# Two wider pads that move every tile of one side of the on-chip memory to a multiple of 256 bytes

## The chip, the cores and the metric

The kernel runs on one core of one Trainium2 chip. The metric is the device time of one execution in microseconds (us), as the median of several runs. Beside the runs there is one profiled execution with its trace; its span runs from the first instruction to the last.

## What is computed

One encoder block over 256 tokens of 2048 channels, in float32. Cut to its shape:

```
h = rmsnorm(x);  proj = h @ w_in                       # 2048 -> 9216
p_hy, p_sgu, g_hy, g_sgu = split(proj)
y_hy  = two long convolutions with implicit filters(p_hy)    # 1024 channels
y_sgu = gelu(u) * (w_s applied along chunks of layernorm(gelu(v)))   # 1024 channels
merged = sigmoid(g_hy) * (y_hy @ w_branch_hyena) + sigmoid(g_sgu) * (y_sgu @ w_branch_sgu)
x = x + merged @ w_out                                 # 2048 -> 2048
gate, up = split(rmsnorm(x) @ w_ffn_in)                # 2048 -> 2 x 5632
x = x + (silu(gate) * up) @ w_ffn_out                  # 5632 -> 2048
out = rmsnorm(x)
```

## The kernel before

**Products in parts.** Every weight is read once from HBM, 512 KB at a time, into a tile `raw` of 128 x 1024 float32. `split_to` makes a rounded part `whi` on ScalarE (line 67) and the rest `wlo` on VectorE (line 68). The activations are held split in the same way: `X`, `M`, `X2`, `H`, `ysgu` and `yhy` hold, for each block k of 128 channels, 256 columns of the rounded part and then 256 of the rest. A product is then three matmuls (lines 132 to 134, in `tokens`): 128 columns of an activation tile are the stationary operand, 512 columns of `whi` or `wlo` are streamed past them. One weight tile gives 12 such matmuls. In the projections u, v, x1 and x2 (`tile16`, lines 98 and 100) it is the other way round: `whi` and `wlo` are stationary, and 512 or 256 columns of `X` are streamed.

**Order of the work.** First the half of the spatial gating that is normalized (lines 700 to 702, 192 matmuls), then the gates (`gate_part`, tiles `mg`, in blocks of 24 matmuls) mixed with `tile16`, the filters and the convolutions (lines 512, 561, 596, 617). After that the two branches (`ysgu`, `yhy`), the output projection (`M`), the first feed-forward product (`X2`, which the profile also calls X) and the second (`H`). `feed` loads and splits the weight tiles ahead of their use, all through SyncE's queue.

**Where tiles lie.** Each of the 128 partitions has one row of addresses. A pool is placed from the left end or, with side="right", from the right end, one behind the other, and every tile is rounded up to 32 bytes. The first tile, `par`, begins at byte 16,512. With the sizes in the code this gives, before the change:

| tiles | side | first byte | past a multiple of 256 |
|---|---|---|---|
| `ones`, `ident` | left | 17,152 | 0 |
| `raw`, `whi`, `wlo` in the pool ws | left | 20,352 | 128 |
| `ysgu` and `X2` (the same place) | left | 80,000 | 128 |
| `yhy` | left | 96,384 | 128 |
| `zh`, `zl` (tokens of the convolution) | left | 120,000 | 192 |
| `w4h`, `w4l`, `fh`, `fl` (filters) | right | 157,504 on | 64 |
| `H` | right | 114,624 | 192 |
| `M` | right | 135,104 | 192 |
| `h3s` | right | 195,520 | 192 |
| `X` | right | 196,544 | 192 |
| `raw`, `whi`, `wlo` in the pool ws2 | right | 204,736 | 192 |

Every operand of a matmul begins a multiple of 512 bytes into its tile, so it lies as far past a multiple of 256 as the tile does. The pool ws2 exists only from the branches on; there every third weight tile of the list goes to it:

```python
            pool, n = (self.ws, RAW_BUFS) if self.ws2 is None or i % 3 else (self.ws2, 2)
```

Of the kernel before, what the change touches and what calls it, by code (L numbers as in the profile page):

```python
# [9 lines left out]
F32 = mybir.dt.float32  # L10
# [6 lines left out]
P = 128  # L17
# [199 lines left out]
def build(nc, tc, a):  # L217
# [29 lines left out]
    with ExitStack() as top:  # L247
        const = top.enter_context(tc.tile_pool(name="const", bufs=1))
# [5 lines left out]

        par = const.tile([P, PC_N], F32, name="par")
        nc.scalar.dma_start(out=par, in_=a["par"])
        const.tile([P, 8], F32, name="const_pad")
        ones = net.ones = const.tile([P, P], F32, name="ones")
        nc.vector.memset(ones, 1.0)
        ident = net.ident = const.tile([P, P], F32, name="ident")  # L260
# [2 lines left out]


        edge = top.enter_context(tc.tile_pool(name="edge", bufs=1, side="right"))
        edge.tile([P, 8], F32, name="edge_pad")
        left = ExitStack()
        ys_pool = left.enter_context(tc.tile_pool(name="ys_pool", bufs=1))
        ysgu = ys_pool.tile([P, 8, 512], F32R, name="ysgu")
# [699 lines left out]
```

## Time and profile before

| what | value |
|---|---|
| time, median of 3 runs | 1407.9 us (1407.68 to 1407.92) |
| time of the profiled execution | 1408.45 us |
| its span | 1406.7 us |
| TensorE busy | 1390.8 us, 99% |
| VectorE, ScalarE busy | 870.1 us, 657.3 us |
| granted TensorE clock, mean | 0.998 |

The trace lists every matmul with its start and a modelled end. Since matmuls are pipelined, the shown duration of one overlaps the next one's; what a matmul costs is the distance from its start to the start of the next.

### The profile page before, as it was taken

Reading aid. Unit: us, or ns where it says so; the run is one execution under the profiler, and the core shown is the slowest. Engines: PE = TensorE matmul, PEld = TensorE weight load, DVE = VectorE, ACT = ScalarE, POOL = GpSimd, SP = SyncE. Lnnn points to the kernel's source line nnn. Section 1 sums busy time; section 2 is a strip of 40 time slices with the busy share of each in tenths; the row PEclk is TensorE's granted clock in tenths of the full one; section 3 lists DMA queues with packets and bytes.
Section 4 is the critical chain, followed back from the end, with each engine's and each line's share of the span. In section 5 each row is a group of like instructions: output and inputs, shape, how many; then the busy total and the mean of one; then the engine's idle time right before and its main releaser. Section 6 shows DMA issues by size and latency. Waiting matters only on the chain.

```text
span 1406.7 us, 17274 instructions
## 1 busy us (share of the span) xinstructions
PE 1390.8 (99%) x6554; PEld 1149.7 (82%) x6554; DVE 870.1 (62%) x1206; ACT 657.3 (47%) x820; POOL 0.7 (0%) x6
## 2 busy tenths in 40 slices
PE   9999999999999999999999999999999999999996
PEld 7888888888888788888888888888888888888885
DVE  7787798797888666556555454545454554545443
ACT  7665555555554444445444444444444443434432
POOL 0000000000000000000000000000000000000000
PEclk9999999999999999999999999999999999999999
DMA  8775656556555786677666566666665667666651
GB/s 285 261 223 180 188 166 199 174 170 205 178 171 165 259 312 183 203 223 209 186 188 186 188 192 184 193 181 190 183 193 184 192 230 234 188 187 193 186 173 60
DMA packets 81170, 276.00 MB, mean 196 GB/s; under 512 B 9016, under 2 KB 9664, under 8 KB 80704
## 3 DMA queue, kind: packets, MB, share of 16 engines
q1 hardware_dynamic: 78064, 269.59, 61.8%
q10 hardware_dynamic: 3024, 5.32, 1.0%
q8 instruction: 51, 0.84, 0.2%
q14 instruction: 31, 0.25, 0.1%
HBM read 266.49 MB, written 8.39 MB: 195 GB/s over the span
## 4 chain that ended last, share of the span: by engine, by line
PE 96%; DMA 1%; DVE 1%; ACT 1%; issue 0%; SPq 0%; ACTq 0%; DVEq 0%
PE mm L132 21%; PE mm L134 21%; PE mm L133 21%; PE mm L98 8%; PE mg L132 4%; PE mg L133 4%; PE mg L134 4%; PE mm L100 4%; PE aux L561 2%; PE aux L160 1%; PE aux L617 1%; PE mm L700 1%; PE mm L701 1%; PE mm L702 1%; PE aux L512 1%; DMA raw<-in_wbr 1%
## 5 line engine op out<-in xcount | busy, mean ns | idle before, releaser
L68 DVE TENSOR_TENSOR wlo<-raw,whi 128x1024 fp32r<-128x1024 f32 (+1 forms) x474 | 577.3, 1219 | 478.1 <-ACT whi L67 474.2
L67 ACT CAST whi<-raw 128x1024 fp32r<-128x1024 f32 (+1 forms) x474 | 495.3, 1046 | 627.1 <-PE mm L134 466.8
L132 PE MATMUL mm<-whi,X 128*128 128x512 f32 x704 | 278.8, 396 | 0.0
L134 PE MATMUL mm<-whi,X 128*128 128x512 f32 x704 | 275.8, 392 | 0.0
L133 PE MATMUL mm<-wlo,X 128*128 128x512 f32 x704 | 274.4, 390 | 0.0
L98 PE MATMUL mm<-X,whi 128*128 128x512 f32 x512 | 160.0, 394 | 0.0
L134 PEld LDWEIGHTS mm<-whi,X 128*128 128x128 f32 x704 | 132.1, 188 | 30.4
L133 PEld LDWEIGHTS mm<-wlo,X 128*128 128x128 f32 x704 | 132.3, 188 | 28.4
L132 PEld LDWEIGHTS mm<-whi,X 128*128 128x128 f32 x704 | 132.2, 188 | 27.2
L133 PE MATMUL mm<-wlo,H 128*128 128x512 f32 x352 | 138.5, 393 | 0.0
L132 PE MATMUL mm<-whi,H 128*128 128x512 f32 x352 | 138.4, 393 | 0.0
L134 PE MATMUL mm<-whi,H 128*128 128x512 f32 x352 | 138.1, 392 | 0.0
L100 PEld LDWEIGHTS mm<-X,wlo 128*128 128x128 f32 x512 | 96.1, 188 | 21.5
L132 PE MATMUL mg<-whi,X 128*128 128x512 f32 x256 | 102.1, 399 | 0.0
L100 PE MATMUL mm<-X,wlo 128*128 128x256 f32 x512 | 101.4, 279 | 0.0
L133 PE MATMUL mg<-wlo,X 128*128 128x512 f32 x256 | 101.1, 395 | 0.0
L134 PE MATMUL mg<-whi,X 128*128 128x512 f32 x256 | 100.9, 395 | 0.0
L98 PEld LDWEIGHTS mm<-X,whi 128*128 128x128 f32 x512 | 78.7, 188 | 1.2
L132 PEld LDWEIGHTS mm<-whi,H 128*128 128x128 f32 x352 | 65.9, 187 | 15.7
L133 PEld LDWEIGHTS mm<-wlo,H 128*128 128x128 f32 x352 | 65.9, 187 | 15.6
L134 PEld LDWEIGHTS mm<-whi,H 128*128 128x128 f32 x352 | 65.9, 187 | 15.5
L134 PEld LDWEIGHTS mg<-whi,X 128*128 128x128 f32 x256 | 48.0, 188 | 11.4
(214 smaller groups left out, 1427.6 us busy)
## 6 DMA issues: line engine op xcount, KB each, us to landing
raw<-in_wfi SPq DMA_DIRECT2D x176, 512.0 KB, 3.5
raw<-in_wfo SPq DMA_DIRECT2D x88, 512.0 KB, 3.5
raw<-in_wg SPq DMA_DIRECT2D x64, 512.0 KB, 3.7
raw<-in_win SPq DMA_DIRECT2D x64, 512.0 KB, 3.9
raw<-in_wbr SPq DMA_DIRECT2D x32, 512.0 KB, 5.7
raw<-in_wout SPq DMA_DIRECT2D x32, 512.0 KB, 4.0
raw<-in_wsv SPq DMA_DIRECT2D x14, 512.0 KB, 5.7
gate_d<-sq ACTq DMA_DIRECT2D x16, 256.0 KB, 5.2
```

What stands on the lines that cost most here:

```text
L67: self.nc.scalar.copy(out=hi, in_=src)
L68: self.nc.vector.tensor_tensor(out=lo, in0=src, in1=hi.bitcast(F32), op=ALU.subtract)
L98: nc.tensor.matmul(ps[:, 0:512], lhsT=hi[:, col:col + P], rhs=mov, start=start, stop=False)
L100: nc.tensor.matmul(ps[:, 0:256], lhsT=lo[:, col:col + P], rhs=mov[:, 0:256], start=False, stop=stop)
L132: self.nc.tensor.matmul(ps[tt], lhsT=xh, rhs=wh, start=start, stop=False)
L133: self.nc.tensor.matmul(ps[tt], lhsT=xh, rhs=wl, start=False, stop=False)
L134: self.nc.tensor.matmul(ps[tt], lhsT=xl, rhs=wh, start=False, stop=stop)
L160: self.nc.tensor.transpose(out=pt[:, b, tt * P:(tt + 1) * P], in_=src[tt][:, cols + b * P:cols + (b + 1) * P], identity=self.ident)
L512: nc.tensor.matmul(ps.rearrange("p d c -> p (d c)"), lhsT=h3s[:, par_ * P:(par_ + 1) * P], rhs=w, start=(part == 0), stop=(part == 1))
L561: nc.tensor.matmul(ps[:, ri, :], lhsT=fw[:, m + ri, :], rhs=z, start=(n == 0), stop=(n == 2))
L617: nc.tensor.matmul(ps[:, ri].rearrange("p h t -> p (h t)"), lhsT=p[:, ri, t * P:(t + 1) * P], rhs=GG[:, 2 * gr + ri, :], start=(n == 0), s ...
L700: nc.tensor.matmul(ps[tt], lhsT=xh, rhs=wh, start=(k == 0), stop=False)
```

## The change

The unused tile behind `par` grows from 32 to 160 bytes, and the unused tile at the right end from 32 to 224 bytes. Everything behind the first moves 128 bytes to the right, everything on the right side 192 bytes to the left. No instruction, tile size, pool or order changes.

```diff
-        const.tile([P, 8], F32, name="const_pad")
+        const.tile([P, 40], F32, name="const_pad")
         ones = net.ones = const.tile([P, P], F32, name="ones")
...
-        edge.tile([P, 8], F32, name="edge_pad")
+        edge.tile([P, 56], F32, name="edge_pad")
```

After it ws, `ysgu`, `X2`, `yhy`, ws2, `H`, `M`, `h3s` and `X` begin at multiples of 256 bytes. `ones` and `ident` then lie 128 past one, the filters' tiles 128, and `zh` and `zl` 64.

## Rows read from the trace of the kernel before

**Rows 1.** The page: TensorE's busy time, and shares of the chain that ended last.

```profile
PE 1390.8 (99%) x6554; PEld 1149.7 (82%) x6554; DVE 870.1 (62%) x1206; ACT 657.3 (47%) x820; POOL 0.7 (0%) x6
...
PE 96%; DMA 1%; DVE 1%; ACT 1%; issue 0%; SPq 0%; ACTq 0%; DVEq 0%
```

**Rows 2.** Stretches: length, busy PE, PEld, DVE, ACT, POOL, clock, DMA share, GB/s.

```profile
0.00:20.00 20.00, 16.83 (x71) 13.02 (x72) 12.88 (x23) 15.46 (x28) 0.70 (x6) 1.00 0.89 296
...
50.00:471.00 421.00, 420.81 (x2268) 359.91 (x2266) 352.51 (x637) 229.03 (x323) 0.00 (x0) 1.00 0.60 184
471.00:485.00 14.00, 12.94 (x57) 10.72 (x58) 5.50 (x5) 5.63 (x6) 0.00 (x0) 1.00 0.99 359
...
656.00:1150.00 494.00, 494.00 (x2203) 405.07 (x2202) 252.98 (x260) 216.93 (x248) 0.00 (x0) 1.00 0.62 188
1150.00:1394.00 244.00, 244.00 (x1057) 197.23 (x1056) 113.43 (x111) 92.74 (x100) 0.00 (x0) 1.00 0.58 182
```

**Rows 3.** Timeline of TensorE, second feed-forward product: start, shown length, instruction.

```profile
1203.84 0.39 PE L132 MATMUL mm<-whi,H 128*128 128x512 f32 x1
...
1206.64 0.39 PE L132 MATMUL mm<-whi,H 128*128 128x512 f32 x1
...
1208.02 0.39 PE L132 MATMUL mm<-whi,H 128*128 128x512 f32 x1
...
1209.38 0.39 PE L132 MATMUL mm<-whi,H 128*128 128x512 f32 x1
...
1212.18 0.39 PE L132 MATMUL mm<-whi,H 128*128 128x512 f32 x1
```

**Rows 4.** Timeline of TensorE, first feed-forward product.

```profile
1004.77 0.40 PE L132 MATMUL mm<-whi,X 128*128 128x512 f32 x1
...
1007.54 0.40 PE L132 MATMUL mm<-whi,X 128*128 128x512 f32 x1
...
1010.31 0.39 PE L132 MATMUL mm<-whi,X 128*128 128x512 f32 x1
...
1013.03 0.40 PE L132 MATMUL mm<-whi,X 128*128 128x512 f32 x1
```

**Rows 5.** Timeline of TensorE, in a block of the gates.

```profile
307.58 0.39 PE L132 MATMUL mg<-whi,X 128*128 128x512 f32 x1
...
310.38 0.39 PE L132 MATMUL mg<-whi,X 128*128 128x512 f32 x1
```

**Rows 6.** Timeline of TensorE, the projections with the weights stationary.

```profile
192.52 0.62 PE L98 MATMUL mm<-X,whi 128*128 128x512 f32 x2
192.97 0.40 PE L100 MATMUL mm<-X,wlo 128*128 128x256 f32 x2
193.21 0.62 PE L98 MATMUL mm<-X,whi 128*128 128x512 f32 x2
193.67 0.39 PE L100 MATMUL mm<-X,wlo 128*128 128x256 f32 x2
193.90 0.62 PE L98 MATMUL mm<-X,whi 128*128 128x512 f32 x2
```

**Rows 7.** Timeline of TensorE, in a filter (line 512), up to the next gate block.

```profile
318.50 0.40 PE L512 MATMUL aux<-w4l,h3s 128*128 128x512 f32 x1
...
319.20 0.39 PE L132 MATMUL mg<-whi,X 128*128 128x512 f32 x1
```

**Rows 8.** Groups by line and form: count, busy us, mean ns.

```profile
L132 PE MATMUL mm<-whi,X 128*128 128x512 f32 x704 | 278.8, 396 | 0.0
...
L98 PE MATMUL mm<-X,whi 128*128 128x512 f32 x512 | 160.0, 394 | 0.0
...
L132 PE MATMUL mm<-whi,H 128*128 128x512 f32 x352 | 138.4, 393 | 0.0
...
L132 PE MATMUL mg<-whi,X 128*128 128x512 f32 x256 | 102.1, 399 | 0.0
...
L132 PEld LDWEIGHTS mm<-whi,H 128*128 128x128 f32 x352 | 65.9, 187 | 15.7
```

## The prediction

> **What bounds the kernel now.** I read the page first. TensorE is busy 1390.8 us of a span of 1406.7 us, and 96% of the chain that ended last is TensorE's own work [rows 1]. The stretches say the same stage by stage: outside the first 20 us and a stretch of 14 us at 471 us, TensorE has no idle time worth the name, at a granted clock of 1.00, which is the 2.4 GHz level, while the DMA share is 0.58 to 0.62 and VectorE, at most, 84% busy (352.5 of 421 us) [rows 2]. Only what changes the distance between one matmul and the next can move the time by per cents.
>
> Next I read the timeline of TensorE for these distances. At 2.4 GHz 512 columns are 213.3 ns, and in the rows below no matmul of 512 columns is that close to the next. One weight tile gives 12 of them, so the starts of tiles are a ruler:
> - In the second feed-forward product a tile of 12 takes 2.80 us (1203.84 to 1206.64), 233.3 ns each. The next takes 2.74 us (to 1209.38), its last six 1.36 us, 226.7 ns each, and the one behind it 2.80 again (to 1212.18) [rows 3]. By line 75 every third tile lies in ws2. The code, the stationary tile H and the instructions are the same; only the place of the streamed tile differs: ws and H lie 128 and 192 past a multiple of 256 bytes, ws2 and H both 192.
> - In the first feed-forward product it is the other way round. X2 lies at 128 as ws does. The tile from ws2 takes 2.77 us, the first from ws after it 2.77, the second 2.72, which is 226.7 ns each [rows 4].
> - The gates stream ws (128) past X (192): 2.80 us for 12, 233.3 ns [rows 5].
> - In a filter a tile at 64 is streamed past one at 192, both on the right side: three distances in 0.70 us, 233.3 ns [rows 7].
>
> So two places (H and X2) with two pools each give a crossed comparison: where streamed and stationary tile lie equally far past a multiple of 256, the distance settles at 226.7 ns; where they differ, it is 229 to 233. After each switch from one sort to the other some 6 to 12 matmuls go by at about 230 before it settles. The load of the next weights (187 ns, [rows 8]) starts together with the matmul before it, so both read the memory at once; that the two reads meet is my reading, the distances are the trace's.
>
> [...]
>
> **The change part by part.** No instruction is added or removed. After it all streamed and stationary tiles of the large products lie at 0, so all are of the equal sort, and no switch between sorts is left. The price of that, tile by tile, with 2.72 us for 12 matmuls everywhere (counts from [rows 8], three lines each, and from the loops of M, the branches and the first stage):
> - H: three tiles take 2.80 + 2.80 + 2.74 = 8.34 us now, 8.16 then; 3 x 352 = 1056 matmuls are 29.3 such threes, so 5.3 us less.
> - M has the same offsets as H: 384 matmuls, 10.7 threes, 1.9 us less.
> - X2: 2.77 + 2.77 + 2.72 = 8.26 us now; 2112 matmuls, 58.7 threes, 0.10 us each, 5.9 us less.
> - The branches (`ysgu` and `yhy` at 128, as X2): 384 matmuls, 1.1 us less.
> - Gates, 768, and the first stage, 192: 80 tiles at 0.08 us, 6.4 us less.
> - Line 98, 512 matmuls with ws stationary (128) and X streamed (192): two pairs take 0.45 and 0.46 us up to the next line, 229 ns on average [rows 6]; at 226.7 that is 1.2 us less.
>
> Together 21.8 us. From this I take off: 1.6 us for the gates, whose 64 blocks of 24 begin behind shorter matmuls (if the first 12 of each took 2.77 us it would be 3.1; I take half, since I don't know which of them disturb it); 1.3 us (192 x 6.6 ns) for the first stage, where TensorE is idle 3.2 of 20 us at a DMA share of 0.89, so that a quicker matmul only waits longer [rows 2]; 0.5 us for the transposes that break into the feed-forward stages. That leaves 18.4 us.
>
> What the trace does not show:
> - The 816 matmuls of 256 columns (as many of line 100 as of line 98, and 304 in filters and convolutions). Some of them get equal offsets, `zh` and `zl` lose theirs. Pairs of line 100 take 0.23 or 0.24 us [rows 6], 115 to 120 ns each; the whole group going to either end is 2.0 us either way. I take nothing.
> - Transfers to better placed rows. TensorE's idle time where the DMA share is 0.89 and 0.99 is 3.2 and 1.1 us [rows 2], so a gain of at most 4.3 us; I see no reason for a loss. I take nothing, since the rows don't say how much of this idle time waits for the transfers themselves.
> - Elementwise work and the transposes, whose identity moves to 128: ScalarE and VectorE have idle time in every long stretch [rows 2], which hides it. That cover would be gone if VectorE's work became 19% slower (421/352.5); from there on what is added would count in full.
>
> [...]
>
> The sum: the profiled execution took 1408.45 us; 1408.45 - 18.4 = 1390.05. The median of the runs is 0.55 us under the profiled one, so I forecast **1390 us**.
>
> **The rivals.**
> 1. *Nothing changes.* The place could matter by something that the pads don't touch, such as how far apart the tiles are: ws with X2 are near, ws2 with H are near, and the others far. Then every distance stays and the time is 1408 us. For it: both feed-forward stages fit as well. Against: [rows 7], where two tiles on the same side, 36 KB apart and 128 out of step, go at 233.3 ns, while ws and X2, which settle at 226.7, are up to 76 KB apart. [...]
> 2. *Far more.* If not only the equality but the boundary itself matters, the distance could fall below 226.7 ns, to 213.3 at the best: 13.4 ns x 5408 = 72 us more, 1318 us. For it: nothing that streams 512 columns lies at 0 now. Against: 128 and 192 settle at the same 226.7.
> 3. *Slower.* With both at 0 the two reads start on the same boundary each time. If they then hold each other up, one more step of 6.7 ns beyond 233.3 would be 240 ns: (240 - 230.8) x 4896 + (240 - 229) x 512 = 51 us more, 1459 us. It decides as soon as the mean exceeds 230.8 ns. Against it: equal offsets at 128 and at 192 are the quickest in the trace.
>
> **How the numbers follow.** A measurement of this kernel tells some 0.2% (2.8 us) from no change. I give the forecast's mechanism, anywhere from 1380 to 1404 us, 0.68 (it goes for four places, and its prices are measured); nothing 0.13; far more 0.08; slower 0.11. The likeliest time is 1390. Its low bound is 1407.9 less all of 21.8, 2.0 and 4.3, which is 1380; upwards the range takes in the first rival with a little of the 256-column bound, 1409. That leaves out rivals 2 and 3, 0.19. So faster 0.68 + 0.08 = 0.76, same 0.13, slower 0.11. The forecast's own range is 1384 (the 3.4 us taken off come after all, and 2.0 from the 256 columns) to 1399 (half of the 18.4 comes).
>
> **What would show it.** In the changed kernel's timeline all three tiles in a row of the H stage and of the X2 stage should take 2.72 us, those of the gates 2.72 to 2.77, the pairs of line 98 0.45. TensorE's busy time should fall by 16 to 20 us and its count stay 6554. If H's tiles from ws stay at 2.80, rival 1 holds; if they drop under 2.70, rival 2; if X2's settled tile rises over 2.77, rival 3. I am wrong, too, if the distances fall as forecast but the time does not, which would need TensorE to begin to wait for `wlo` or for DMA between 50 and 471 us.

## The result, and the profile after

The changed kernel takes 1392.9 us (median of 4 runs, 1392.78 to 1393.29); the kernel before, beside it, 1407.85 us (1407.68 to 1407.92). The ratio is 0.9895, with an interval of 0.9877 to 0.9912. That is 14.9 us less, where 18 were forecast (1390 us, range 1380 to 1409). The profiled execution took 1393.07 us, its span is 1391.3 us, so 15.4 us less than the span before.

The page after, busy time and count of each engine:

```profile
PE 1375.7 (99%) x6554; PEld 1151.0 (83%) x6554; DVE 869.8 (63%) x1206; ACT 658.5 (47%) x820; POOL 0.7 (0%) x6
```

TensorE does the same 6554 matmuls in 15.1 us less; the work of every other engine is within 1.2 us of what it was [rows 1]. The stretches after (columns as in [rows 2]):

```profile
0.00:20.00 20.00, 17.09 (x71) 13.39 (x72) 12.62 (x22) 15.42 (x28) 0.70 (x6) 1.00 0.86 302
...
650.00:1139.00 489.00, 489.00 (x2201) 404.57 (x2200) 252.46 (x260) 217.28 (x248) 0.00 (x0) 1.00 0.62 190
1140.00:1378.00 238.00, 238.00 (x1053) 197.05 (x1053) 112.70 (x108) 93.05 (x100) 0.00 (x0) 1.00 0.59 186
```

The granted clock is 1.00 on both sides, so no part of the gain is clock, and in the two long stages TensorE is without a gap as before, so no part of it is waiting. About as many matmuls as took 494 and 244 us [rows 2] take 489 and 238.

Where the time came from is read best from line 132, the first of the three matmuls of a product. Its rows give count, shortest, median and longest shown length in ns, and the first and last start. Before:

```profile
L132 PE MATMUL mm<-whi,X x704: 388/394/486, 656.0 to 1149.9; 128*128 128x512 f32 x176
...
L132 PE MATMUL mm<-whi,H x352: 388/394/476, 1150.5 to 1395.0; 128*128 128x512 f32 x176
...
L132 PE MATMUL mg<-whi,X x256: 388/394/584, 55.4 to 469.9; 128*128 128x512 f32 x128
...
L132 PE MATMUL mm<-whi,M x128: 388/394/483, 563.4 to 655.3; 128*128 128x512 f32 x128
```

After:

```profile
L132 PE MATMUL mm<-whi,X x704: 389/389/486, 650.2 to 1139.6; 128*128 128x512 f32 x176
...
L132 PE MATMUL mm<-whi,H x352: 389/389/486, 1140.3 to 1379.4; 128*128 128x512 f32 x176
...
L132 PE MATMUL mg<-whi,X x256: 387/389/585, 54.8 to 466.9; 128*128 128x512 f32 x128
...
L132 PE MATMUL mm<-whi,M x128: 389/389/486, 559.1 to 649.5; 128*128 128x512 f32 x128
```

Last start less first start is the length of a stage: X2 from 493.9 to 489.4 us (-4.5), H from 244.5 to 239.1 (-5.4), M from 91.9 to 90.4 (-1.5). The gates stretch, which holds lines 98 and 100, the filters and the convolutions too, goes from 414.5 to 412.1 (-2.4), what precedes it is 0.6 us shorter, and what lies between the gates and M, the branches above all, 1.3 us. The medians tell it as well: the middle value of 394 ns is now 389 everywhere.

In the timeline after, tiles of 12 matmuls follow each other evenly. A tile of the gates, three tiles in a row of X2 and three of H:

```profile
307.06 0.39 PE L132 MATMUL mg<-whi,X 128*128 128x512 f32 x1
...
309.78 0.39 PE L132 MATMUL mg<-whi,X 128*128 128x512 f32 x1
...
995.17 0.39 PE L132 MATMUL mm<-whi,X 128*128 128x512 f32 x1
...
1003.33 0.39 PE L132 MATMUL mm<-whi,X 128*128 128x512 f32 x1
...
1189.72 0.39 PE L132 MATMUL mm<-whi,H 128*128 128x512 f32 x1
...
1192.44 0.39 PE L132 MATMUL mm<-whi,H 128*128 128x512 f32 x1
...
1195.16 0.39 PE L132 MATMUL mm<-whi,H 128*128 128x512 f32 x1
...
1197.88 0.39 PE L132 MATMUL mm<-whi,H 128*128 128x512 f32 x1
```

H takes 2.72, 2.72 and 2.72 us where it took 2.80, 2.74 and 2.80 [rows 3]; X2 takes 8.16 us for 36 where it took 8.26 [rows 4]; the gates 2.72 where they took 2.80 [rows 5]. 2.72 us for 12 is 226.7 ns.

### The profile page after: what moved, and what is told of

It reads as the page before. It is cut to its first block, busy times and chain, and to the rows that moved or that the text cites. A ratio compares the mean times of both kernels' runs of the same rounds, so it can differ in the third digit from the quotient of the medians.

```text
span 1391.3 us, 17274 instructions
## 1 busy us (share of the span) xinstructions
PE 1375.7 (99%) x6554; PEld 1151.0 (83%) x6554; DVE 869.8 (63%) x1206; ACT 658.5 (47%) x820; POOL 0.7 (0%) x6
## 4 chain that ended last, share of the span: by engine, by line
PE 97%; DVE 1%; ACT 1%; DMA 0%; issue 0%; SPq 0%; ACTq 0%
PE mm L132 21%; PE mm L134 21%; PE mm L133 21%; PE mm L98 9%; PE mm L100 4%; PE mg L132 4%; PE mg L134 4%; PE mg L133 4%; PE aux L561 2%; PE aux L160 1%; PE aux L617 1%; PE aux L512 1%; PE mm L700 1%; PE mm L702 1%; PE mm L701 1%; PE aux L596 0%
## 5 line engine op out<-in xcount | busy, mean ns | idle before, releaser
L132 PEld LDWEIGHTS mm<-whi,H 128*128 128x128 f32 x352 | 66.1, 188 | 13.7
L134 PEld LDWEIGHTS mg<-whi,X 128*128 128x128 f32 x256 | 48.1, 188 | 10.2
```

Of the source, the lines that this page charges most:

```text
L132: self.nc.tensor.matmul(ps[tt], lhsT=xh, rhs=wh, start=start, stop=False)
L134: self.nc.tensor.matmul(ps[tt], lhsT=xl, rhs=wh, start=False, stop=stop)
```

## The experiments

In what follows the place of a tile is the number of bytes by which it lies past a multiple of 256, and the distance is that from the start of one matmul to the start of the next.

### Is it the boundary, or that both operands lie equally far past it?

**Everything at 128.** Both pads chosen so that the same tiles lie 128 past a multiple of 256:

```diff
-        const.tile([P, 40], F32, name="const_pad")
+        const.tile([P, 8], F32, name="const_pad")
...
-        edge.tile([P, 56], F32, name="edge_pad")
+        edge.tile([P, 24], F32, name="edge_pad")
```

> Left pad as before, right pad 96 bytes: all streamed and stationary tiles of the large products lie 128 past a multiple of 256, none on it. Theory A (only the difference of the two places modulo 256 counts): the same distances as in the changed kernel, 226.7 ns in H and X2, time 1393 (1391 to 1395). Theory B (the boundary itself counts): no or half the gain, 1400 to 1410. Theory C (how far apart the tiles lie counts, the pads do not): 1408, which the changed kernel has already spoken against.

Measured: 1393.36 us (1393.02 to 1393.69), ratio 0.9897 (0.9882 to 0.9911), the changed kernel's time to 0.5 us. Three tiles of H, timeline:

```profile
1195.23 0.39 PE L132 MATMUL mm<-whi,H 128*128 128x512 f32 x1
...
1203.39 0.39 PE L132 MATMUL mm<-whi,H 128*128 128x512 f32 x1
```

8.16 us for 36, as after the change. No tile of the large products lies on a multiple of 256 here, and the whole gain is there. The boundary by itself is worth nothing. That holds for the transfers too: every weight row starts 128 bytes past a multiple of 256 here and on one in the changed kernel, and the two times differ by 0.4 us, within what a measurement tells.

**The left pad alone, the right pad alone.** The tiles of one side at 0, those of the other as before (in the first, left 0 and right 192; in the second, left 128 and right 0):

```diff
-        edge.tile([P, 56], F32, name="edge_pad")
+        edge.tile([P, 8], F32, name="edge_pad")
```

```diff
-        const.tile([P, 40], F32, name="const_pad")
+        const.tile([P, 8], F32, name="const_pad")
```

> Left side at 0, right side stays at 192: the signs of the differences change, ws against H, M and X becomes +64, ws2 against X2 becomes -64. Theory A: tiles of H and of the gates from ws settle near 229 ns (now 233.3), tiles of X2 from ws2 rise from 230 to 233.3: about 5 us less than before, 1402 (1399 to 1406), and line 98 (X 64 behind ws) may add or take 2. Theory B: the left operands have their gain whatever the right ones do, 226.7 ns where both are left (X2 with ws) as before and half of the gain elsewhere, 1397 to 1402, the same for this and for the right pad alone.

> Left side stays at 128, right side at 0: the differences become 128 modulo 256. Theory A with the price of the filter's row (128 out of step: 233.3 ns): H, M and gates from ws stay at 233.3, X2 from ws2 rises from 230 to 233.3, together 2 us more than before, 1410 (1407 to 1413). Theory B: half of the gain, as for the left pad alone, 1397 to 1402.

Measured: the left pad alone 1403.77 us (1403.51 to 1404.49), ratio 0.997 (0.9959 to 0.9981); the right pad alone 1408.55 us (1408.05 to 1409.73), ratio 1.0005 (0.9996 to 1.0015). The H stage, with the left pad alone:

```profile
1194.94 0.40 PE L132 MATMUL mm<-whi,H 128*128 128x512 f32 x1
...
1203.22 0.40 PE L132 MATMUL mm<-whi,H 128*128 128x512 f32 x1
```

With the right pad alone:

```profile
1195.37 0.40 PE L132 MATMUL mm<-whi,H 128*128 128x512 f32 x1
...
1198.17 0.39 PE L132 MATMUL mm<-whi,H 128*128 128x512 f32 x1
...
1200.90 0.40 PE L132 MATMUL mm<-whi,H 128*128 128x512 f32 x1
...
1203.70 0.40 PE L132 MATMUL mm<-whi,H 128*128 128x512 f32 x1
```

With the right pad alone H and ws2 lie at 0, ws at 128: 2.80, 2.73 and 2.80 us, the pattern of before. That a third of the tiles lies on the boundary together with H changes nothing against [rows 3], where it lay with H at 192. With the left pad alone the three tiles take 8.28 us. There ws lies at 0 and H at 192, so the streamed tile is 64 further on, and the mean distance of such matmuls (ws with the gates' X, M and H, without those next to another sort of matmul) is 229.5 ns, not 233.3: at this one distance in place the cost is smaller. The 36 take 8.28 us, a little more than the 8.26 of 36 such matmuls; one tile in three comes from ws2, and after a switch the first matmuls are slower (in [rows 3] the first six of such a tile take 1.38 us, the last six 1.36). The two gains (4.1 us and none) don't add up to that of both (14.9 us): it is the pair of places that counts.

**32 bytes out of step.** Left at 0, right at 32:

```diff
-        edge.tile([P, 56], F32, name="edge_pad")
+        edge.tile([P, 48], F32, name="edge_pad")
```

> Left side at 0, right side 32 past a multiple of 256, the smallest step that the allocator makes. Theory A has no price for it: if the distance goes in steps of 64 bytes, either all stays at 226.7 ns (1393) or goes as with 64 (1400 to 1408); if it is gradual, near 230 ns (about 1400). Theory B: the left operands keep their gain, 1397 to 1402.

Measured: 1410.06 us (1409.77 to 1410.64), ratio 1.0016 (1.0006 to 1.0025). None of the times that were expected came (1393, 1400 to 1408, about 1400, 1397 to 1402): a matmul pays as much for 32 bytes as for 128. Counted as above, the mean with the streamed tile at 0 and the stationary one at 32 is 233.1 ns, and that with the places exchanged (X2 with ws2) 233.6.

**H alone 64 further on.** The changed kernel with one unused tile in H's pool, which moves H (and no other operand of a matmul) by 192 bytes, from place 0 to 64:

```diff
         H = hpool.tile([P, NF, 512], F32R, name="H")
+        hpool.tile([P, 48], F32, name="h_pad")
```

> The changed kernel with H alone moved back by 192 bytes, to 64 past a multiple of 256, everything else equal. Theory A: the 1056 matmuls of the second feed-forward product go from 226.7 to 233.3 ns, 7.0 us more, 1400; no other stage changes. Rival (the time follows from the whole layout, not from each pair of operands): less than 3 us, or other stages change too.

Measured: 1399.49 us (1399.23 to 1399.85), ratio 0.9941 (0.9926 to 0.9956), 6.3 us more than the changed kernel beside it (below). Line 132:

```profile
L132 PE MATMUL mm<-whi,X x704: 389/389/486, 649.9 to 1139.3; 128*128 128x512 f32 x176
...
L132 PE MATMUL mm<-whi,H x352: 393/396/478, 1140.0 to 1386.1; 128*128 128x512 f32 x176
```

The X2 stage is 489.4 us long as after the change, H 246.1 in place of 239.1. All of the loss lies in the one stage whose stationary tile was moved, with every other operand of a matmul where it was. Seen from the streamed tile, 192 further on costs 6.6 ns (7.0 us over 1056 matmuls; 6.5 of them are left in the span); in the left pad's run 64 further on cost 2.9 ns.

### How does the cost go with the places, and is it TensorE alone?

A kernel of long series on fixed tiles, W streamed and A stationary, in the order of lines 132 to 134, 120 matmuls a series; the first number is the place of W in floats, the second that of A:

```python
SERIES = [("sa", 0, 0), ("sb", 1, 0), ("sc", 2, 0), ("sd", 4, 0), ("se", 8, 0), ("sf", 16, 0), ("sg", 24, 0), ("sh", 32, 0),
          ("si", 40, 0), ("sj", 48, 0), ("sk", 56, 0), ("sl", 60, 0), ("sm", 62, 0), ("sn", 63, 0),
          ("ta", 0, 8), ("tb", 0, 16), ("tc", 4, 4), ("td", 8, 8)]
MORE = [("ua", 0, 0, 512, 64), ("ub", 8, 0, 512, 64), ("uc", 0, 0, 512, 32), ("ud", 8, 0, 512, 32),
        ("va", 0, 0, 256, P), ("vb", 8, 0, 256, P)]
```

> Leaves out the whole block: it runs nothing but series of 120 matmuls each in the order of lines 132 to 134, on tiles that are loaded once, with no other engine at work, and writes the last sums out. One series for each distance in bytes of the streamed operand behind the stationary one (0, 4, 8, 16, 32, 64, 96, 128, 160, 192, 224, 240, 248, 252, and -32, -64), two with both moved by 16 and by 32, four with only 64 or 32 stationary columns, two with 256 streamed columns. Theory A: 226.7 ns at 0 wherever both lie, 229 to 233.5 at 32, 64, 128 and 192, whether or not other engines work. Rival (it is the other engines' or the transfers' accesses that meet TensorE's): all series alike. If the 13.4 ns above 213.3 come from the load of the next weights, 64 and 32 stationary columns should bring the distance to some 220 and 217 ns; if they are a fixed cost of each matmul, it stays 226.7.

Measured: 722.34 us, one run. Timeline of TensorE, each series a row (start, length of the series, tiles, columns):

```profile
39.05 27.36 PE L42 MATMUL sa<-W,A 128*128 128x512 f32 x120
66.25 28.69 PE L42 MATMUL sb<-W,A 128*128 128x512 f32 x120
...
150.70 28.16 PE L42 MATMUL se<-W,A 128*128 128x512 f32 x120
178.70 27.64 PE L42 MATMUL sf<-W,A 128*128 128x512 f32 x120
...
234.19 28.16 PE L42 MATMUL sh<-W,A 128*128 128x512 f32 x120
...
402.29 27.51 PE L42 MATMUL sn<-W,A 128*128 128x512 f32 x120
429.64 28.16 PE L42 MATMUL ta<-W,A 128*128 128x512 f32 x120
...
485.64 27.90 PE L42 MATMUL tc<-W,A 128*128 128x512 f32 x120
513.38 27.37 PE L42 MATMUL td<-W,A 128*128 128x512 f32 x120
540.58 27.76 PE L42 MATMUL ua<-W,A 128*64 128x512 f32 x120
...
595.89 27.96 PE L42 MATMUL uc<-W,A 128*32 128x512 f32 x120
...
651.66 14.55 PE L42 MATMUL va<-W,A 128*128 128x256 f32 x120
666.05 14.30 PE L42 MATMUL vb<-W,A 128*128 128x256 f32 x120
```

And the stretch with all of them (columns as in [rows 2]):

```profile
39.00:700.00 661.00, 661.00 (x2969) 509.02 (x2969) 0.00 (x0) 0.00 (x0) 0.00 (x0) 1.00 0.00 1
```

Each series' length reaches 0.16 us into the next one (39.05 + 27.36 - 66.25); less that, and by 120, it is the mean distance. So equal places (`sa`) give 27.20/120 = 226.7 ns, W 32 bytes further on (`se`) 233.3, 64 (`sf`) 229.0, 128 (`sh`) 233.3, A 32 further on (`ta`) 233.3. The seven series between 96 and 248 bytes, `sh` among them, lie at 233.3 to 234.2. Both at 32 (`td`) are as fast as both at 0; both at 16 bytes (`tc`) take 231.2. These are the kernel's numbers with no transfer, no other engine and no moving buffer beside the matmuls, at a granted clock of 1.00: the effect is TensorE's own with the two places.

The series with fewer stationary columns test my reading that the load of the next weights meets the streamed read. A tile of 64 or of 32 columns (`ua`, `uc`) is less to load, yet takes 230.0 and 231.7 ns at equal places, more than the 226.7 of the full one. Neither the 220 and 217 ns of the reading nor the 226.7 of a fixed cost came. That gives the reading no support, though it doesn't rule out that the two reads meet in another way; what it is in TensorE that the places act on stays open.

At 256 columns it is the other way round: equal places take 119.9 ns (`va`), 32 bytes apart 117.8 (`vb`).

### Where did the forecast gain of line 98 go?

The distances of line 98 summed over the whole trace rise from 118.4 to 119.9 us, and those of line 100, which alternates with it, fall from 59.7 to 59.3: +1.2 us together, where -1.2 was forecast. A second kernel of series put the question alone: pairs of 512 and 256 columns as lines 98 and 100 issue them (places of X, `whi`, `wlo`, in floats), and single lengths (place of W, of A, columns):

```python
PAIRS = [("pa", 0, 0, 0), ("pb", 0, 56, 56), ("pc", 0, 48, 48), ("pd", 0, 40, 40), ("pe", 0, 32, 32), ("pf", 0, 24, 24),
         ("pg", 0, 16, 16), ("ph", 0, 8, 8), ("qa", 0, 56, 0), ("qb", 0, 48, 0), ("qc", 0, 32, 0), ("qd", 0, 16, 0),
         ("qe", 0, 0, 56), ("qf", 0, 0, 48), ("qg", 0, 0, 32), ("qh", 0, 0, 16)]
MORE = [("ca", 0, 0, 128, P), ("cb", 0, 0, 256, P), ("cc", 0, 0, 384, P), ("cd", 0, 0, 512, P),
        ("da", 32, 0, 128, P), ("db", 32, 0, 256, P), ("dc", 32, 0, 384, P), ("dd", 32, 0, 512, P),
        ("ea", 32, 32, 512, P), ("eb", 2, 2, 512, P), ("ec", 16, 0, 256, P), ("ed", 48, 0, 256, P)]
```

> Leaves out the whole block, as the first measurement of distances alone did. Sixteen series of 128 matmuls in the order of lines 98 and 100 (two of 512 columns, two of 256), with whi and wlo of the stationary side at different places and the streamed one at 0; then series in the order of lines 132 to 134 with 128, 256, 384 and 512 streamed columns, at equal places and 128 apart, and both operands 128 or 8 bytes past a multiple of 256. If line 98 depends on its own distance alone, the order of the sixteen series follows the order of whi's places whatever wlo does; if it depends on the alternation with the shorter line 100, equal places are not the best ones here, since pairs at 0 took 349 ns (234.3 + 115.8 less, on average) in the changed kernel and 229 + 117 in the one before. If the cost above the streaming time (13.3 ns at equal places for 512 and for 256 columns) is fixed for each matmul, 128 and 384 columns show 13.3 ns too at equal places; if it grows with the columns, 384 show 10.

Measured: 674.88 us, one run. Timeline of TensorE:

```profile
39.06 22.45 PE L55 MATMUL pa<-W,A 128*128 128x512 f32 x128
61.34 22.36 PE L55 MATMUL pb<-W,A 128*128 128x512 f32 x128
83.55 22.27 PE L55 MATMUL pc<-W,A 128*128 128x512 f32 x128
...
284.72 22.98 PE L55 MATMUL qd<-W,A 128*128 128x512 f32 x128
...
410.28 14.60 PE L42 MATMUL cb<-W,A 128*128 128x256 f32 x120
424.72 20.97 PE L42 MATMUL cc<-W,A 128*128 128x384 f32 x120
445.53 27.40 PE L42 MATMUL cd<-W,A 128*128 128x512 f32 x120
...
486.11 14.45 PE L42 MATMUL db<-W,A 128*128 128x256 f32 x120
500.41 21.28 PE L42 MATMUL dc<-W,A 128*128 128x384 f32 x120
521.53 28.16 PE L42 MATMUL dd<-W,A 128*128 128x512 f32 x120
```

Read in the same way, by 128 for the pairs, the mean distance is 174.1 ns at equal places (`pa`), 173.5 with X 32 further on (`pb`), 172.7 with X 64 further on (`pc`) and at the worst 178.3 (`qd`). `pc` is how X (192) and ws (128) lay before the change: line 98 had the best of these sixteen places already, and the change put it where 1024 matmuls cost 1.4 ns more each, 1.4 us in all. The kernel shows +1.2. It isn't the place of `whi` alone that counts: with `whi` at 64 in both, the mean is 178.3 ns with `wlo` at 0 (`qd`) and 173.5 with `wlo` at 64 too (`pg`).

The lengths show where equality begins to help. At equal places 256 columns take 120.3 ns (`cb`) and 512 take 227.0 (`cd`), so 256 columns more cost 106.7 ns (106.8 in the first series, `va` and `sa`): 0.417 ns a column, or 2.4 columns a ns at a granted clock of 1.00, the rate behind the prediction's 2.4 GHz and its 213.3 ns for 512 columns. The part above the columns' own time at this rate (106.7, 160.0 and 213.3 ns) is 13.4 to 13.7 ns at 256, 384 and 512 columns (`cb`, `cc`, `cd`: 120.3, 173.4 and 227.0 ns). 128 bytes apart it grows: 12.5, 16.0 and 20.0 ns (`db`, `dc`, `dd`: 119.2, 176.0 and 233.3 ns). The two cross between 256 and 384 columns. The part is no fixed cost of every matmul, though: 128 columns take 111.2 ns at either place (`ca`, `da`), 57.9 above the 53.3 of their columns at the same rate.

**Giving line 98 its distance back.** With the changed kernel's pads, the `win` tiles alone are written further on in slightly longer buffers. First only `whi`, by 224 bytes, so that X is 32 further on in line 98; then `whi` and `wlo` by 192 bytes, X 64 further on in both lines, as before the change. The room for it comes from one buffer of `hb` less and, the second time, from `sqs`, which moves to another pool. The edit of the second (the first has 56 in place of 48 and leaves `wlo` and `sqs` as they were):

```diff
+                o = 48 if i in self.off else 0
-                hi = pool.tile([P, 1024], F32R, name="whi", bufs=n)[:, 0:w]
-                lo = pool.tile([P, 1024], F32R, name="wlo", bufs=n)[:, 0:w]
+                hi = pool.tile([P, 1024 + 64 * (pool is self.ws)], F32R, name="whi", bufs=n)[:, o:o + w]
+                lo = pool.tile([P, 1024 + 64 * (pool is self.ws)], F32R, name="wlo", bufs=n)[:, o:o + w]
...
             tile_first.append(net.chunk(a["win"][col0[t[0]] + t[1]]))
+            net.off.update((tile_first[-1], tile_first[-1] + 1))
...
-    sqs = const.tile([P, L], F32, name="sqs")
+    sqs = ev.tile([P, L], F32, name="evb", bufs=2)
...
-        hb = aux.tile([1, CB], F32, name="hb", bufs=2)
+        hb = aux.tile([1, CB], F32, name="hb", bufs=1)
```

> The changed kernel, with whi of the projections u, v, x1 and x2 written 224 bytes into a slightly longer tile (one buffer less of the filter's bias makes room), so that line 98 has X 32 bytes past its stationary tile, the best distance that the five kernels have shown for it (230.6 ns on average against 234.3 at 0), while lines 132 to 134 stay at 0. Theory A: 512 x 3.7 ns = 1.9 us less than the changed kernel, 1391. Rival (line 98 depends on what runs around it, not on its own distance): no change, 1393.

> The changed kernel, with whi and wlo of the projections u, v, x1 and x2 both written 192 bytes into slightly longer tiles, so that lines 98 and 100 have X 64 bytes past the stationary tile, as they had before the change; lines 132 to 134 stay at 0. The room comes from the filter's bias (one buffer less) and from a sum of squares that now lies in another pool. If the series of pairs hold in the kernel (172.5 ns per matmul 64 apart, 174.3 at 0), 1024 x 1.8 ns = 1.9 us less than the changed kernel, 1391.2, and 1.0 us less than the version with whi alone 32 apart. Rival (the series don't carry over): 1393.

Beside them the changed kernel ran again, once with each:

> The changed kernel once more, beside the others on the same chip: 1393.

> The changed kernel as it is, beside the version with the pairs 64 apart on the same chip, so that the two can be compared: 1393.1.

Measured: with `whi` alone 1392.29 us (1392.1 to 1392.4) beside 1393.15 for the changed kernel (1392.96 to 1393.26); with both 1392.2 us (1392.02 to 1392.32) beside 1392.95 (1392.76 to 1393.16). One whole block of 32 matmuls of lines 98 and 100, from its first start to the first of what follows. Before:

```profile
192.52 0.62 PE L98 MATMUL mm<-X,whi 128*128 128x512 f32 x2
...
198.04 0.28 PE L561 MATMUL aux<-fh,Fh 128*128 128x256 f32 x1
```

After:

```profile
177.71 0.63 PE L98 MATMUL mm<-X,whi 128*128 128x512 f32 x2
...
183.31 0.27 PE L810 MATMUL aux<-ident,sd 128*128 128x128 f32 x1
```

With `whi` and `wlo` moved (its lines are numbered two or three higher here):

```profile
177.69 0.63 PE L100 MATMUL mm<-X,whi 128*128 128x512 f32 x2
...
183.24 0.38 PE L813 MATMUL aux<-ident,sd 128*128 128x128 f32 x2
```

5.52, 5.60 and 5.55 us, one block of many. Over all 1024 matmuls of the two lines the sums are 178.0 before, 179.2 after, 178.5 with `whi` alone moved and 178.0 with both: the whole 1.2 us come back in the second. Of these 0.75 us reach the time (1392.95 to 1392.2). In the two traces taken beside each other the first stage takes 1.0 us more with both moved (48.1 for 47.1 us) and the warm-up matmuls ahead of it 0.4 less (3.9 for 4.3). The first stage varies by 0.6 us between the three traces of the changed kernel itself (47.1 to 47.7), so how much of that is the edit's isn't shown. Either version was expected to take 1.9 us less than the changed kernel; with `whi` alone it is 0.86 us, and the two lines give 0.7. Against the kernel before, these two are the fastest of all here, ratio 0.9889 (0.9875 to 0.9904 and 0.9874 to 0.9904). They are 0.05 to 0.06% below the changed kernel, less than the 0.2% that a measurement tells; their runs don't overlap with those of the changed kernel beside them, but no more than that is claimed.

## Why the prediction was right, and where it missed

The mechanism was the one forecast: equal places of streamed and stationary tile give 226.7 ns, at 0 as at 128 and 192. The tiles of H, X2 and the gates show it as forecast; TensorE's busy time fell by 15.1 us, a little less than the 16 to 20 given, and the pairs of line 98 take 0.46 to 0.47 us in the block shown above, not 0.45. Point by point, with each term's measured size from the sum of all distances of its matmuls in the two traces:

| step | forecast | measured |
|---|---|---|
| H | -5.3 | -5.3 |
| M | -1.9 | -1.6 |
| X2, with 0.5 off for all transposes | -5.4 | -4.4 |
| branches | -1.1 | -1.1 |
| gates, with 1.6 off | -3.5 | -3.7 |
| first stage, with 1.3 off | 0 | -1.2 |
| lines 98 and 100 | -1.2 | +1.2 |
| warm-up matmuls ahead of the first stage | 0 | +0.4 |
| filters, convolutions, transposes | 0 | +0.1 |
| sum | -18.4 | -15.6 |

- **Line 98 is the term with the wrong sign**, 2.4 us of the 2.8 that are missing. I took 226.7 ns for it, a price of series in which one length follows itself. Line 98 alternates with 256 columns, and for such pairs 64 bytes apart is the best place and equality a middling one (172.7 and 174.1 ns). The term was also misread: the 0.91 us for four matmuls in [rows 6] are 227.5 ns each, not 229, so these rows left 0.4 us to gain, not 1.2; over the whole trace line 98 went from 231.2 to 234.3 ns. No row had a pair at equal places, so the 226.7 for it was carried over from another order of matmuls.
- **X2** gave 1.0 less. Its undisturbed matmuls, those more than 24 behind a group of transposes, went from 229.2 to 226.7 ns; I had used 229.4. The first 12 matmuls behind each of 23 such groups gained nothing (the first of each 316 ns before and 318 after, the other eleven 230.1 and 230.9 on average), and the gain counted for them, 276 times 2.7 ns or 0.75 us, is more than the 0.5 us set aside.
- **The gates** came out by luck. The 1.6 us taken off are half of a loss in 64 blocks of 24 matmuls; 768 matmuls are only 32 such blocks. Rightly counted, half would have been 0.8 and the whole 1.6, and nearly the whole was lost: 64 of the 80 tiles, 5.1 us, less the 3.7 measured is 1.4.
- **The first stage** gave 1.2 us where nothing was forecast. Between the three traces of the changed kernel it varies from 47.1 to 47.7 us (48.5 before), and the warm-up ahead of it takes 0.3 to 0.5 us more in them than before, so 0.5 to 0.9 us of gain are left. TensorE's idle time in the first 20 us went from 3.2 us to 2.9 (2.8 and 2.0 in the other two), so the quicker matmuls there did not just wait. That the sum missed by no more than 2.8 us is owed to this part too.
- **What was taken at nothing** (256 columns, transposes with the identity at 128, faster transfers) came to +0.1 us; the transposes with the identity cost what they did (13.46 and 13.43 us at line 160). The +0.4 us of the warm-up are no cost of its tiles' place: before, its matmuls are from the second on 213 ns apart up to 4.4 us, from where the trace has the full clock granted, and 111 behind that; in the changed kernel the trace has it from 5.3 us on (5.0 and 5.7 in the other two traces), and up to there they are 213 apart. The elementwise work stayed covered: TensorE is without a gap in the long stages. The transfers' places gave next to nothing, as everything at 128 shows (0.4 us between rows on the boundary and 128 past it): the 4.3 us that the low end of the range, 1380, counts for better placed rows are TensorE's idle time before, and no run shows a gain of that kind.
- **Rival 1** (nothing changes) falls with the result, and its condition with the experiments: moving H alone by 192 bytes costs 7.0 us in its stage, so it is not which side or how far apart the tiles are; 6.6 ns a matmul hang on the places.
- **Rival 2** (far more on the boundary) falls with everything at 128: 1393.4 us, and no large product settled below 226.7 ns in either kernel; its 213.3 ns are 512 columns at the 0.417 ns that `cb` and `cd` show for one, with nothing above them.
- **Rival 3** (240 ns at equal places on the boundary) falls with the H rows after, 226.7 ns. The 230.8 ns it counts from are the mean of the 4896 matmuls before: 2496 at 8.26/36 us, 1440 at 8.34/36 and 960 at 233.3 ns.
- **"The two reads meet"**, given as my reading, has no support: fewer stationary columns made the matmul at equal places slower, not faster. The forecast did not rest on it, since it used the distances only.

## What to carry to other kernels

Where long series of matmuls of 512 columns in this format (`F32R` in the code) set the time, place the streamed and the stationary tile equally far past a multiple of 256 bytes (and on a multiple of 32); here it was worth 2.9% of such a matmul against most other places (226.7 ns for 233.3), and which common place it is made no difference at 0, 32, 128 and 192 (226.7 ns at each). Check every pool, since one tile out of step by 32 bytes pays in full (233.1 and 233.6 ns in the kernel). Products of 256 columns, or of 512 and 256 in turn, want another distance (32 bytes gave 117.8 for 119.9 ns in the first, 64 bytes 172.7 for 174.1 in the second): price each kind of product in its own order, not by its neighbour's.

## What the runs showed of the hardware that was not expected

- The cost does not grow with the distance: 32 bytes out of step cost the same 6.7 ns as 128, 64 bytes only 2.3 (226.7 at equal places, then 233.3, 233.3 and 229.0 ns).
- 4 bytes out of step cost most of all places tried: 237.8 ns (`sb`), 11.1 ns above equality. But 252, which is 4 bytes short of the next equality, costs 1.2 (`sn`, 227.9).
- Below 32 bytes the common place matters too: both at 16 bytes 231.2 ns (`tc`), both at 32 bytes 226.7 (`td`).
- Narrower weights are not cheaper here: 128, 64 and 32 stationary columns take 226.7, 230.0 and 231.7 ns at equal places (`sa`, `ua`, `uc`).
- At equal places the cost above streaming is the same 13.5 ns, within 0.2, at 256, 384 and 512 columns; 128 bytes apart it grows from 12.5 to 20.0 ns.
